# Low halves of all raw weights made by ScalarE and an adding transfer, and a recurrent branch with its steps in another order

## The chip, the cores and the metric

The kernel runs on one core of a Trainium2 chip. It uses TensorE (PE, with its weight loads shown apart as PEld), VectorE (DVE), ScalarE (ACT), GpSimd (POOL) and SyncE (SP). The metric is the device time of one launch in microseconds (us). Less is better.

## The reference, cut to what matters

One block of a decoder, in float32, over 1024 tokens and 16 meta tokens with 1024 features:

```
u = rms_norm(h)
q, k, v, r, a_lr, c_in, g_gla, g_conf = split(u @ w_in)      # 4 heads of 128 keys, 256 values
log_a = log_sigmoid(a_lr @ w_alpha_up + b_alpha) / 16
# recurrent branch, per head:
#   S_t = diag(exp(log_a_t)) S_{t-1} + k_t^T v_t ;  o_t = q_t S_t
o = rms_norm(o) * silu(r);                 br_gla  = o @ w_gla_o
c = silu(layer_norm(dwconv31(c1 * sigmoid(c2))));   br_conf = c @ w_conf_o
h = h + (sigmoid(g_gla) * br_gla + sigmoid(g_conf) * br_conf) @ w_out
a, b = split(rms_norm(h) @ w_up)                              # 2 x 2816
h = h + (silu(dwconv3(a)) * b) @ w_down
out = rms_norm(h)
```

Inside a chunk of tokens the recurrent branch needs the scores q_i k_j weighted by the decay between j and i. The kernel makes them by levels: at the level s, blocks of 2s tokens are taken, and the right half of each block (queries) meets the left half (keys), both scaled by the decay to the middle of the block.

## The kernel before, in words

**Three passes for one product.** Every large product is computed with numbers of reduced width. Each operand is the sum of a rounded part (high) and the rest (low), and a product takes three passes into the same accumulator: high weight by high activation (L187), high weight by low activation (L188), low weight by high activation (L189). Weights pass through as pieces of 128 x 1024 (512 KB), some of 512 or 768 columns: SP loads the raw piece (three buffers, `load_raw`), ACT rounds it into `wh` (L161, L174), and the rest goes to `wl`. The pairs `wh`, `wl` have three buffers too, so that a piece can be split only when the piece three before it has been used up.

**Two ways to the low half.** `split_w` subtracts on DVE (L162), or on POOL where it is asked to. The first 51 pieces of `w_mix` go another way (`load_w` with `PO`): ACT writes the rounded piece with its sign turned into `wl` (L173), and a transfer started by POOL adds the raw piece from memory to it (L175). POOL spends some 0.88 us on starting one.

**Stages.** From 0 to 740 us the 57 pieces of `w_mix` are multiplied; between these products, a count of steps per block (`tick`) lets the generators `gla` (recurrent branch, one head after the other), the convolution (most of DVE's work, L370) and later the layer norm advance. To 832 us come gate products and the layer norm. Then `w_gla_o` and `w_conf_o` follow (16 pieces, 11.3 us each), and from 1014 us `w_out` (8 pieces, twice, for two halves of the tokens, 5.7 us each). In the second half of `w_out`, the first half's tokens are normalised and become operands (`normalise`, `operand`; the low part on POOL, L228). The up-projection follows from 1108 us: 22 units, each with the pieces r1 and r2 of 1024 columns. A unit's two half-size blocks are combined by a fast multiplication scheme: sums of raw weights are made on POOL (L765 to L768) into `Pt` and r1, and the four pairs that a unit uses are `w1` (raw r1, for units from the fifth on), `w21` (from `Pt`), `w34` (from the changed r1; POOL subtracts from the fifth unit on) and the second half `a22` of r2. From 1577 us `w_down` closes the kernel: 24 pieces for each half of the tokens, with the units' results read back from memory by transfers that POOL starts (`ar`, L871) and split anew.

**What sets the order.** A scheduler places instructions in the order of the program, moved forward by `high_priority` for weights; each engine then goes through its row in order, and an instruction that waits holds back those behind it. That holds for the transfers that POOL starts as well.

**The recurrent branch.** Per head, `gla` makes the decays, then for each level s of 64, 32, 16 (band: L485, one product for each block) and 8, 4, 2, 1 (fine: L507, one 128 x 128 product for each of 8 chunks) the scaled tile `E` (`level`: subtraction on DVE for the keys L469 and POOL for the queries L470, an exponential on ACT, multiplication on DVE L472 and POOL L473). The product of a level stands one step behind its `level`. Fine products keep only the marked elements (`copy_predicated`, L511, one for each chunk). Then eight chunks follow one after the other: output, state, next chunk.

Of the kernel before, what the change touches and what calls it, by code (L numbers as in the profile page):

```python
# [11 lines left out]
F32R = mybir.dt.float32r  # L12
# [4 lines left out]
P = 128  # L17
# [47 lines left out]
def build(ctx, tc, xT, w_mix, w_o3, w_up, w_dn, w_au, pvec, masks, outT):  # L65
# [43 lines left out]
    def tmp512():  # L109
        return small([P, 520], "t512", bufs=6)  # L110
# [45 lines left out]
    def split_w(raw, eng=None):  # L156
        uid[0] += 1
        n = raw.shape[-1]
        hi = wspl.tile([P, 1024], F32R, tag="hi", name=f"wh_{uid[0]}")[:, :n]
        lo = wspl.tile([P, 1024], F32R, tag="lo", name=f"wl_{uid[0]}")[:, :n]  # L160
        pin(S.activation(hi, raw, AF.Copy))  # L161
        (eng or V).tensor_tensor(lo, raw, hi.bitcast(F32), op=ALU.subtract)  # L162
        return hi, lo

    def load_w(src, eng=None, ahead=4000):
        with tc.high_priority(offset=ahead):
            raw = load_raw(src)
            if eng is not PO:
                return split_w(raw, eng)
            uid[0] += 1  # L170
            hi = wspl.tile([P, 1024], F32R, tag="hi", name=f"wh_{uid[0]}")
            lo = wspl.tile([P, 1024], F32R, tag="lo", name=f"wl_{uid[0]}")
            pin(S.activation(lo, raw, AF.Copy, scale=-1.0))  # L173
            pin(S.activation(hi, raw, AF.Copy))  # L174
            nc.gpsimd.dma_start(lo, src, accum_op=ALU.add)  # L175
            return hi, lo
# [213 lines left out]
    def gla(h, q, k, vt):  # L390
# [32 lines left out]
        qd = slot(nm="qd")  # L423
        S.activation(qd[:, :SEQ], np_, AF.Exp, scale=-1.0 / TAU)
        V.memset(qd[:, :SEQ].rearrange("p (c t) -> p c t", t=CH)[:, :, 0:1], 1.0)
        V.tensor_tensor(qd[:, :SEQ], qd[:, :SEQ], qx, op=ALU.mult)
        yield 1
        km = small([P, 32], "km")
# [5 lines left out]
        pm = psumg()  # L434
        PE.matmul(pm[:15, 0:1], km[:, 16:31], q[:, 0:1], start=True, stop=True)
        PE.transpose(pm[:16, P : 2 * P], km[:, 0:16], ident)
        pms = small([16, 2], "pms")
        V.memset(pms, 0.0)  # L438
        V.tensor_copy(pms[:15, 0:1], pm[:15, 0:1])
# [3 lines left out]
        kmT = small([16, P], "kmT", bufs=1)  # L443
        S.activation(kmT, pm[:16, P : 2 * P], AF.Copy)
        po = psumg()
        PE.matmul(po[:, :DVH], kmT, vmeta, start=True, stop=True)
        st = small([P, DVH], "st", bufs=3)
        V.tensor_copy(st, po[:, :DVH])
        ss = small([P, NCH + 1], "ss")
        V.memset(ss, 1.0)  # L450
        yield 1
        kdT = slot(nm="kdT")
        for c4 in range(2):
            pt = psumg()
            for e in range(4):
                c = c4 * 4 + e
                PE.transpose(pt[:, e * P : (e + 1) * P], kd[:, c * CH : (c + 1) * CH], ident)
            S.activation(kdT[:, c4 * 512 : c4 * 512 + 512], pt, AF.Copy)
            yield 1
# [17 lines left out]
        for s in BANDS:  # L477
            X = level(s)
            yield 1
# [7 lines left out]
            for b in range(64 // s):  # L487
# [5 lines left out]
                else:  # L493
                    V.tensor_copy(dst, src)
            yield 1
        for n, s in enumerate(FINE):
            if s > 1:
                X = level(s)
                yield 1
                lt, rt = X, X  # L500
            else:
                lt, rt = kx, qx
            for c4 in range(2):
                pt = psumg()
                for e in range(4):
# [513 lines left out]
```

## Time and profile before

| what | value |
|---|---|
| median of 3 runs | 1852.41 us (1851.85 to 1853.7) |
| the profiled execution, its own time | 1854.06 us |
| its span, first to last instruction | 1852.3 us |
| mean granted TensorE clock | 0.989 of full speed |
| PE / DVE / ACT / POOL busy | 96% / 63% / 38% / 25% |
| DVE subtractions for `wl` (L162) | 134 instructions, 157.9 us |
| DMA share over the span | 26.6% (loads and stores by SP and ACT), 10.1% (started by POOL) |

How to read it: a busy share belongs to the whole span; what counts is where PE waits, since PE is busy for 1772.4 of 1852.3 us. An engine that is busy for less of the time than PE can still be the one that PE waits for, in one stage. The transfers have their own limit: the DMA share says how busy the core's 16 DMA engines were in a stretch.

### The profile page before, as it was taken

The numbers are of one execution on the slowest core, as the hardware profiler recorded it, in microseconds if no ns is written. First come the engines' busy times: TensorE is split into PE (matmuls) and PEld (weight loads), VectorE is DVE, ScalarE is ACT, GpSimd is POOL, SyncE is SP. The second block draws the span as 40 slices with busy tenths as digits, with TensorE's granted clock in tenths as the row PEclk, the third lists the DMA queues.
The fourth block names the chain that finished last, engine by engine and source line by source line (L and its number), as shares of the span: only waits on it lengthen the run. The fifth ranks groups of instructions, "written<-read, shape, count | busy, mean of one in ns | idle before, by whom it ended". The sixth has DMA issues, their size and how long they took to land.

```text
span 1852.3 us, 29073 instructions
## 1 busy us (share of the span) xinstructions
PE 1772.4 (96%) x12210; PEld 1688.0 (91%) x12210; DVE 1164.0 (63%) x1462; ACT 707.8 (38%) x1052; POOL 458.2 (25%) x333
## 2 busy tenths in 40 slices
PE   4999999999999999999999997999999999899997
PEld 3999899999899898999999997999999999677886
DVE  5239958969896761634365369877667766733523
ACT  5326426526435744592222343222222223423321
POOL 2102313413413422200000255433333334200000
PEclk8999999999999999999999998999999999999999
DMA  6343335244334553554133541221221224644532
GB/s 210 75 94 84 68 80 117 62 96 103 69 80 103 132 115 86 170 176 154 46 109 129 185 127 46 92 80 69 88 84 69 81 89 142 216 117 147 161 121 66
DMA packets 63443, 200.94 MB, mean 108 GB/s; under 512 B 6864, under 2 KB 14160, under 8 KB 63312
## 3 DMA queue, kind: packets, MB, share of 16 engines
q1 hardware_dynamic: 51168, 159.03, 26.6%
q0 software_dynamic: 10368, 37.75, 10.1%
q10 hardware_dynamic: 1776, 2.30, 0.4%
q8 instruction: 96, 1.57, 0.4%
q14 instruction: 35, 0.29, 0.0%
HBM read 162.31 MB, written 36.74 MB: 107 GB/s over the span
## 4 chain that ended last, share of the span: by engine, by line
PE 54%; DVE 5%; DMA 1%; issue 1%; ACT 1%; POOL 0%; DVEq 0%; ACTq 0%
PE prod L187 12%; PE prod L189 12%; PE prod L188 12%; PE mm L188 6%; PE mm L187 6%; PE mm L189 6%; DVE opl L228 1%; DVE wl L162 1%; DVE un L722 1%; DMA ar<-act_d 1%; PE g L943 1%; DMA wr<-in_w_dn 1%; DVE un L840 0%; DVE fy L825 0%; POOL opl L228 0%
## 5 line engine op out<-in xcount | busy, mean ns | idle before, releaser
L187 PE MATMUL mm<-uh,wh 128*128 128x342 f32 (+4 forms) x1344 | 444.8, 331 | 0.0
L188 PE MATMUL mm<-ul,wh 128*128 128x342 f32 (+4 forms) x1344 | 433.7, 323 | 0.0
L189 PE MATMUL mm<-uh,wl 128*128 128x342 f32 (+4 forms) x1344 | 432.1, 322 | 0.0
L188 PE MATMUL prod<-opl,wh 128*128 128x258 f32 x1232 | 350.2, 284 | 12.6 <-DVE opl L228 12.2
L187 PE MATMUL prod<-oph,wh 128*128 128x258 f32 x1232 | 350.5, 285 | 4.6 <-DVE t L805 3.5
L189 PE MATMUL prod<-oph,wl 128*128 128x258 f32 x1232 | 350.7, 285 | 0.0
L370 DVE SCALAR_TENSOR_TENSOR y<-c,pv,y 128x1026 f32<-128x1026 f32 x240 | 341.7, 1424 | 5.4 <-DVE pms L438 0.3
L161 ACT ACTIVATE wh<-wr 128x1024 fp32r<-128x1024 f32 (+2 forms) x152 | 147.8, 975 | 382.3 <-PE prod L188 175.3
L162 DVE TENSOR_TENSOR wl<-wr,wh 128x1024 fp32r<-128x1024 f32 (+2 forms) x134 | 157.9, 1181 | 176.4 <-ACT wh L161 175.1
L187 PEld LDWEIGHTS mm<-uh,wh 128*128 128x128 f32 x1344 | 255.0, 190 | 4.1 <-issue 2.1
L188 PEld LDWEIGHTS mm<-ul,wh 128*128 128x128 f32 x1344 | 254.7, 190 | 3.1 <-issue 2.1
L189 PEld LDWEIGHTS mm<-uh,wl 128*128 128x128 f32 x1344 | 255.1, 190 | 0.6 <-issue 0.3
L188 PEld LDWEIGHTS prod<-opl,wh 128*128 128x128 f32 x1232 | 235.1, 191 | 13.8 <-DVE opl L228 13.1
L187 PEld LDWEIGHTS prod<-oph,wh 128*128 128x128 f32 x1232 | 235.0, 191 | 5.7 <-issue 3.2
L189 PEld LDWEIGHTS prod<-oph,wl 128*128 128x128 f32 x1232 | 234.9, 191 | 0.0
L189 PE MATMUL mm<-oph,wl 128*128 128x512 f32 (+1 forms) x374 | 143.3, 384 | 4.2 <-DVE wl L162 4.2
L187 PE MATMUL mm<-oph,wh 128*128 128x512 f32 (+1 forms) x374 | 143.5, 384 | 2.1 <-ACT wh L161 1.3
L188 PE MATMUL mm<-opl,wh 128*128 128x512 f32 (+1 forms) x374 | 144.3, 386 | 0.6 <-DVE opl L228 0.6
L187 PE MATMUL prod<-sh,wh 128*128 128x342 f32 (+2 forms) x448 | 133.8, 299 | 0.5 <-ACT gate L629 0.5
L188 PE MATMUL prod<-sl,wh 128*128 128x342 f32 (+2 forms) x448 | 133.7, 298 | 0.0
L189 PE MATMUL prod<-sh,wl 128*128 128x342 f32 (+2 forms) x448 | 133.4, 298 | 0.0
L175 POOL DMA_DIRECT2D wl<-in_w_mix x50 | 43.8, 877 | 306.7 <-ACT wl L173 306.5
(239 smaller groups left out, 2873.2 us busy)
## 6 DMA issues: line engine op xcount, KB each, us to landing
wr<-in_w_mix SPq DMA_DIRECT2D x56, 512.0 KB, 3.9
wl<-in_w_mix POOLq DMA_DIRECT2D x50, 512.0 KB, 7.8
wr<-in_w_up SPq DMA_DIRECT2D x48, 512.0 KB, 3.3
wr<-in_w_o SPq DMA_DIRECT2D x32, 512.0 KB, 3.6
wr<-in_w_dn SPq DMA_DIRECT2D x32, 512.0 KB, 3.6
act_d<-fy SPq DMA_DIRECT2D x21, 512.0 KB, 2.6
ar<-act_d POOLq DMA_DIRECT2D x21, 512.0 KB, 6.9
wr<-in_w_dn SPq DMA_DIRECT2D x16, 384.0 KB, 3.1
```

Of the source, the lines that this page charges most:

```text
L161: pin(S.activation(hi, raw, AF.Copy))
L162: (eng or V).tensor_tensor(lo, raw, hi.bitcast(F32), op=ALU.subtract)
L175: nc.gpsimd.dma_start(lo, src, accum_op=ALU.add)
L187: PE.matmul(out, whi[:, wk], hi[:, c0:c1], start=first and k == 0, stop=False)
L188: PE.matmul(out, whi[:, wk], lo[:, c0:c1], start=False, stop=False)
L189: PE.matmul(out, wlo[:, wk], hi[:, c0:c1], start=False, stop=last and k == n - 1)
L228: (eng or V).tensor_tensor(lo, src, hi.bitcast(F32), op=ALU.subtract)
L370: V.scalar_tensor_tensor(y[:, :LQ], c[:, j : j + LQ], pcol("dw_w", i * CONV_K + j), y[:, :LQ], op0=ALU.mult, op1=ALU.add)
L722: V.scalar_tensor_tensor(pair_cols(un[hf][j], 0, width)[:, e], pair_cols(hh[j], 0, width)[:, e], pcol("ffn_g", 2 * j + e), rs[:, :width], ...
L943: PE.matmul(stats[c], ones, sq, start=n == 1, stop=n == KT - 1)
```

## The change

**Weights.** `load_w` now takes the second way for every piece. A new function `split_from` holds it: negated rounding and rounding on ACT (2 activations), then the adding transfer started by POOL. Besides all of `w_mix` it serves `w_gla_o`, `w_conf_o`, `w_out`, all pieces of `w_down`, and, in the up-projection, `w1` and `a22`, which are raw. `w21` and `w34` hold sums of weights and are still subtracted. In numbers of instructions DVE goes from 1160 rows to 1008, ACT from 1013 to 1142, POOL from 330 to 460; PE has 11332 for 11328.

**The recurrent branch.** `level` now runs some steps ahead of the product that uses it; the tile `qd` is made late; in the row of chunks the state advances two chunks ahead of the outputs. The fine products take only the 64 columns that count as the moving operand, the eight chunks share one bank, and one `copy_predicated` takes the place of eight.

```diff
-    def split_w(raw, eng=None):
+    def weight_pair(n):
         uid[0] += 1
-        n = raw.shape[-1]
         hi = wspl.tile([P, 1024], F32R, tag="hi", name=f"wh_{uid[0]}")[:, :n]
         lo = wspl.tile([P, 1024], F32R, tag="lo", name=f"wl_{uid[0]}")[:, :n]
+        return hi, lo
+
+    def split_w(raw, eng=None):
+        hi, lo = weight_pair(raw.shape[-1])
         pin(S.activation(hi, raw, AF.Copy))
         (eng or V).tensor_tensor(lo, raw, hi.bitcast(F32), op=ALU.subtract)
         return hi, lo
 
-    def load_w(src, eng=None, ahead=4000):
+    def split_from(src, raw):
+        hi, lo = weight_pair(raw.shape[-1])
+        pin(S.activation(lo, raw, AF.Copy, scale=-1.0))
+        pin(S.activation(hi, raw, AF.Copy))
+        nc.gpsimd.dma_start(lo, src, accum_op=ALU.add)
+        return hi, lo
+
+    def load_w(src, ahead=4000):
         with tc.high_priority(offset=ahead):
-            raw = load_raw(src)
-            if eng is not PO:
-                return split_w(raw, eng)
...
+            return split_from(src, load_raw(src))
...
-            wq.append(load_alpha(src) if src is w_alpha else load_w(src, PO if wpos[0] < 51 else V, rate["ahead"]))
+            wq.append(load_alpha(src) if src is w_alpha else load_w(src, rate["ahead"]))
...
+        def fine(n, s, lt, rt):
+            pt = psumg()
+            half = CH // 2
+            for c in range(NCH):
+                sl = slice(c * CH, (c + 1) * CH)
+                PE.matmul(pt[:, c * half : (c + 1) * half].rearrange("p (b t) -> p b t", t=s), lt[:, sl],
+                          right(rt[:, sl], s), start=True, stop=True)
+            mk = right(msk[:, n * CH : (n + 1) * CH], s).rearrange("p (o b) t -> p o b t", o=1)
+            V.copy_predicated(
+                Pc.rearrange("p c (b t) -> p c b t", t=2 * s)[:, :, :, s : 2 * s],
+                mk.broadcast_to([P, NCH, half // s, s]),
+                pt.rearrange("p (c b t) -> p c b t", t=s, b=half // s))
+
+        x64 = level(64)
...
+        x32 = level(32)
...
+        band(64, x64)
+        yield 1
+        x16 = level(16)
+        yield 1
+        band(32, x32)
...
+        x = level(8)
+        yield 1
+        band(16, x16)
+        yield 1
+        for n, s in enumerate(FINE[:-1]):
+            nxt = level(FINE[n + 1]) if n < 2 else None
+            yield 1
+            fine(n, s, x, x)
+            x = nxt
+            yield 1
...
+        for c in range(NCH + 2):
+            if c >= 2:
+                output(c - 2)
+            if c < NCH:
+                advance(c)
             yield 1
...
-            w1 = None if f < HEADS_UP else split_w(r1)
+            w1 = None if f < HEADS_UP else split_from(w_up[f], r1)
...
-            return w1, w21, w34, split_w(a22)
+            return w1, w21, w34, split_from(w_up[FT + f][:, 512:], a22)
```

**How instructions move: DVE in the recurrent branch.** First DVE's row before, where one head's levels 64, 32 and 16 (`E` of 128x8x64, 128x16x32, 128x32x16) are made among the convolution's steps (`y`), with the band products copied into `Pt`:

```order
L469 TENSOR_TENSOR E_2837<-nb_2525 128x8x64
L469 TENSOR_TENSOR E_2882<-nb_2525 128x16x32
...
L472 TENSOR_TENSOR E_2882<-E_2882,k_1139 128x16x32
L370 SCALAR_TENSOR_TENSOR y_2888<-c_1954,pv,y_2888 128x1026 x4
L494 COPY Pt<-g_2872 64x8x64
L370 SCALAR_TENSOR_TENSOR y_2888<-c_1954,pv,y_2888 128x1026 x3
L494 COPY Pt<-g_2925 32x8x32
L469 TENSOR_TENSOR E_2972<-nb_2525 128x32x16
L469 TENSOR_TENSOR E_3043<-nb_2525 128x64x8
L370 SCALAR_TENSOR_TENSOR y_2888<-c_1954,pv,y_2888 128x1026
L472 TENSOR_TENSOR E_2972<-E_2972,k_1139 128x32x16
```

And the same place of the changed kernel:

```order
L443 TENSOR_TENSOR E_2765<-nb_2493 128x16x32
...
L443 TENSOR_TENSOR E_2846<-nb_2493 128x32x16
L368 TENSOR_SCALAR y_2877<-c_1960,pv 128x1026
L446 TENSOR_TENSOR E_2765<-E_2765,k_1139 128x16x32
L371 SCALAR_TENSOR_TENSOR y_2877<-c_1960,pv,y_2877 128x1026
L446 TENSOR_TENSOR E_2846<-E_2846,k_1139 128x32x16
L371 SCALAR_TENSOR_TENSOR y_2877<-c_1960,pv,y_2877 128x1026
L467 COPY Pt<-g_2807 64x8x64
L371 SCALAR_TENSOR_TENSOR y_2877<-c_1960,pv,y_2877 128x1026 x3
L467 COPY Pt<-g_2852 32x8x32
```

The tile of level 16 stood behind the copies of levels 64 and 32; now it is made ahead of both.

**POOL in the last up-projection unit and at the entry to `w_down`.** Before, the unit's sums (`Pt`, `wr`) and its subtraction, then the read-back transfers `ar` in one row, and two low halves of activations (`opl`):

```order
L768 TENSOR_TENSOR wr_14796<-wr_14796,Pt 128x512
L162 TENSOR_TENSOR wl_14813<-wr_14796,wh_14812 128x1024
L871 DMA ar_15205<-act_d_10272 128x2x512
...
L871 DMA ar_15265<-act_d_10280 128x2x512
L228 TENSOR_TENSOR opl_15268<-ar_15265,oph_15267 128x1024
L871 DMA ar_15271<-act_d_10281 128x2x512
L228 TENSOR_TENSOR opl_15274<-ar_15271,oph_15273 128x1024
```

And in the changed kernel, from the same sums on:

```order
L796 TENSOR_TENSOR wr_14748<-wr_14748,Pt 128x512
L165 TENSOR_TENSOR wl_14766<-wr_14748,wh_14765 128x1024
L172 DMA wl_14770<-in_w_up 128x512
L899 DMA ar_15159<-act_d_10182 128x2x512
...
L172 DMA wl_15174<-in_w_dn 128x1024
...
L172 DMA wl_15205<-in_w_dn 128x1024
L899 DMA ar_15215<-act_d_10189 128x2x512
L899 DMA ar_15221<-act_d_10190 128x2x512
L229 TENSOR_TENSOR opl_15224<-ar_15221,oph_15223 128x1024
L899 DMA ar_15227<-act_d_10191 128x2x512
L229 TENSOR_TENSOR opl_15230<-ar_15227,oph_15229 128x1024
L172 DMA wl_15236<-in_w_dn 128x1024
```

The adding transfers of the first two pieces of `w_down` stand between the read-backs, and that of the third behind both subtractions of activations.

## Rows read from the trace of the kernel before

**Rows 1.** PE's waits: what for, total us, times, longest us.
```profile
PE prod L188 <- DVE opl L228: 12.2, 4, 6.2
PE g L485 <- POOL E L473: 10.0, 4, 4.6
...
PE g L550 <- DVE t L544: 4.6, 4, 1.7
PE mm L189 <- DVE wl L162: 4.2, 3, 1.9
PE prod L187 <- DVE t L805: 3.5, 4, 0.9
...
PE g L507 <- DVE E L472: 2.6, 2, 1.7
PE g L435 <- DVE km L433: 1.4, 1, 1.4
```

**Rows 2.** Window behind a recurrent wait: busy PE, PEld, DVE, ACT, POOL, PEclk, DMA.
```profile
200.00:204.00 4.00, 4.00 (x76) 3.96 (x77) 3.96 (x4) 0.27 (x1) 4.00 (x3) 0.57 0.59 146
```

**Rows 3.** PE's instructions: start, duration, engine, line, what.
```profile
31.39 0.41 PE L189 MATMUL mm<-uh,wl 128*128 128x242 f32 x1
31.60 0.41 PE L187 MATMUL mm<-uh,wh 128*128 128x242 f32 x1
...
206.05 1.05 PE L507 MATMUL g<-E 128*128 128x128 f32 x8
```

**Rows 4.** Adding transfer by itself: POOL's start of it, its landing after that.
```profile
L175 POOL DMA_DIRECT2D wl<-in_w_mix x1: 862/862/862, 170.5 to 170.5; - x1
...
DMA to landing us min/median/max: 5.2/5.2/5.2
```

**Rows 5.** The same beside a raw load, and the page's medians (section 6).
```profile
L175 POOL DMA_DIRECT2D wl<-in_w_mix x1: 880/880/880, 184.0 to 184.0; - x1
...
DMA to landing us min/median/max: 7.9/7.9/7.9
...
wl<-in_w_mix POOLq DMA_DIRECT2D x50, 512.0 KB, 7.8
```

**Rows 6.** ACT and a window (columns as Rows 2) at the entry to w_gla_o.
```profile
837.80 1.99 ACT L161 ACTIVATE wh<-wr 128x1024 fp32r<-128x1024 f32 x2
...
840.00:845.00 5.00, 5.00 (x34) 5.00 (x34) 3.37 (x6) 1.06 (x1) 0.00 (x0) 1.00 0.94 308
```

**Rows 7.** POOL and PE while the first half is normalised inside w_out.
```profile
1081.46 5.79 POOL L228 TENSOR_TENSOR opl<-un,oph 128x1032 fp32r<-128x1032 f32 x2 [1.74 <-ACT oph L227]
...
1085.45 0.36 PE L187 MATMUL prod<-mh,wh 128*128 128x258 f32 x1 [0.36 <-DVE hh L745]
```

**Rows 8.** ACT in one up-projection unit, and DMA of the same stretch.
```profile
1406.23 1.06 ACT L161 ACTIVATE wh<-wr 128x1024 fp32r<-128x1024 f32 x1 [2.27 <-PE prod L188]
...
1414.86 1.06 ACT L161 ACTIVATE wh<-wr 128x1024 fp32r<-128x1024 f32 x1 [1.77 <-PE prod L188]
...
1409.00:1411.00 2.00, 2.00 (x19) 2.00 (x18) 1.39 (x2) 0.00 (x0) 2.00 (x2) 1.00 0.00 0
```

**Rows 9.** Entry to w_down: read-backs' landings (first nine; tenth), POOL, PE.
```profile
DMA to landing us min/median/max: 5.4/8.9/11.3
...
DMA to landing us min/median/max: 4.2/4.2/4.2
...
1572.72 0.72 POOL L871 DMA_DIRECT2D ar<-act_d  x1 [2.03 <-PE prod L188]
1581.38 3.35 POOL L228 TENSOR_TENSOR opl<-ar,oph 128x1024 fp32r<-128x1024 f32 x1 [7.94 <-ACT oph L227]
...
1596.95 0.50 PE L189 MATMUL mm<-oph,wl 128*128 128x512 f32 x1 [1.90 <-DVE wl L162]
```

**Rows 10.** ACT in w_down: each start follows the end of a 768-column piece.
```profile
1641.25 1.06 ACT L161 ACTIVATE wh<-wr 128x1024 fp32r<-128x1024 f32 x1 [4.75 <-PE mm L188]
1645.38 1.06 ACT L161 ACTIVATE wh<-wr 128x1024 fp32r<-128x1024 f32 x1 [3.07 <-PE mm L188]
```

More of the change, by code (lines that the diff above doesn't have):

```diff
@@ L476, in gla, with band @@
         Pc = Pt.rearrange("p (c t) -> p c t", t=CH)
-        for s in BANDS:
-            X = level(s)
-            yield 1
+        def band(s, X):
             pt = psumg()
@@ L494, in gla, with right @@
                     V.tensor_copy(dst, src)
[L495 to L514 removed]
+        def right(t, s):
+            return t.rearrange("p (b t) -> p b t", t=2 * s)[:, :, s : 2 * s]
@@ new lines, in gla @@
+        x64 = level(64)
+        kdT = slot(nm="kdT")
+        for c4 in range(2):
+            pt = psumg()
+            for e in range(4):
+                c = c4 * 4 + e
+                PE.transpose(pt[:, e * P : (e + 1) * P], kd[:, c * CH : (c + 1) * CH], ident)
+            S.activation(kdT[:, c4 * 512 : c4 * 512 + 512], pt, AF.Copy)
+            yield 1
+        x32 = level(32)
+        pm = psumg()
+        PE.matmul(pm[:15, 0:1], km[:, 16:31], q[:, 0:1], start=True, stop=True)
+        PE.transpose(pm[:16, P : 2 * P], km[:, 0:16], ident)
@@ new lines, in gla @@
+        pms = small([16, 2], "pms")
+        V.memset(pms, 0.0)
+        V.tensor_copy(pms[:15, 0:1], pm[:15, 0:1])
+        kmT = small([16, P], "kmT", bufs=1)
+        S.activation(kmT, pm[:16, P : 2 * P], AF.Copy)
+        yield 1
[4 more added lines that the diff above has]
+        band(32, x32)
+        po = psumg()
+        PE.matmul(po[:, :DVH], kmT, vmeta, start=True, stop=True)
+        st = small([P, DVH], "st", bufs=4)
+        V.tensor_copy(st, po[:, :DVH])
@@ L516, in gla, with advance @@
+        V.tensor_tensor(qd[:, :SEQ], qd[:, :SEQ], qx, op=ALU.mult)
+        fine(3, 1, kx, qx)
+        yield 1
         o = [slot(nm="o"), slot(nm="o")]
-        for c in range(NCH):
-            op = psumg()
-            PE.matmul(op[:, :DVH], qd[:, c * CH : (c + 1) * CH], st, start=True, stop=False)
-            PE.matmul(op[:, :DVH], Pt[:, c * CH : (c + 1) * CH], vc(c), start=False, stop=True)
+        sts = [st]
+        def advance(c):
             kv_ps = psumg()
             PE.matmul(kv_ps[:, :DVH], kdT[:, c * CH : (c + 1) * CH], vc(c), start=True, stop=True)
-            st2 = small([P, DVH], "st", bufs=3)
-            V.scalar_tensor_tensor(st2, st, dec[:, c : c + 1], kv_ps[:, :DVH], op0=ALU.mult, op1=ALU.add)
-            st = st2
+            st2 = small([P, DVH], "st", bufs=4)
+            V.scalar_tensor_tensor(st2, sts[-1], dec[:, c : c + 1], kv_ps[:, :DVH], op0=ALU.mult, op1=ALU.add)
+            sts.append(st2)
@@ L526, in gla, with output @@
+        def output(c):
+            op = psumg()
+            PE.matmul(op[:, :DVH], qd[:, c * CH : (c + 1) * CH], sts[c], start=True, stop=False)
+            PE.matmul(op[:, :DVH], Pt[:, c * CH : (c + 1) * CH], vc(c), start=False, stop=True)
             oc = o[c // 4][:, (c % 4) * DVH : (c % 4 + 1) * DVH]
@@ L545, in gla @@
         yield 1
+        yield 1
         for d in range(2):
@@ L556, in gla @@
                 S.activation(og[:, 1 + c4 * 512 : 1 + c4 * 512 + 512], pt, AF.Copy, scale=gcol)
+            pt = psumg()
+            PE.transpose(pt[:, 0:2], om[:, d * P : (d + 1) * P], ident[:2, :2])
+            S.activation(og[:, 0 : LQ : LQ - 1], pt[:, 0:2], AF.Copy, scale=gcol)
             ogs[2 * h + d] = og
```

59 lines of the change are left out of this document (10 added, 49 removed).

## Prediction

> **What bounds the kernel now.** The page's first part says PE: busy for 1772.4 of 1852.3 us, at a clock that was granted almost in full. A gain can only come out of PE's waits, or of fewer or shorter passes; a loss comes from each piece of weights whose low half arrives after PE asks for it. So I read the list of PE's waits first [rows 1]. The recurrent branch holds four of them (L485, L550, L507, L435): 10.0 + 4.6 + 2.6 + 1.4 = 18.6 us. The entry to the up-projection holds 12.2 us behind the low halves of activations (L228), its first units 3.5 us (L805). The waits for `wl` itself, which is what the change moves off DVE, come to 4.2 us in all, three of them, all at the entry to `w_down`. So the low halves are nearly free today. The reader is to see that 130 subtractions leave an engine that PE hardly waits for, and that what replaces them has a longer way.
>
> That way is priced next. A DVE subtraction of a 1024-column piece takes some 1.2 us after `wh`. The adding transfer, already in use for most of `w_mix`, lands 5.2 us after its start when nothing else moves [rows 4], 7.9 us beside a raw load, and 7.8 us in the median of 50 [rows 5]. In `w_mix` a piece is used for over 11 us and this is hidden. Elsewhere I go through the stages one by one and ask when the low half is wanted.
>
> **Recurrent branch.** Making the level tiles earlier takes away the wait for `E` (10.0 + 2.6), and the late moves of `km` and the output's tail take away most of the other 6.0. Behind the longest of these waits the clock stood at 0.57 for 4 us [rows 2]; 0.43 x 4 = 1.7 us came back late there and would be saved too. At most this is 18.6 + 1.7 = 20.3 us. I take -15, since POOL makes half of each `E` in 2.3 us steps and has no fewer of them, and the chunks' own chain keeps some of its waits. Ends: -20 and -8 (only L485's waits go).
>
> **Fine products.** 128 products (four heads, four levels, eight chunks) of 128 columns become 128 of 64. In float32 each is two passes, 256 in all. Eight passes take 1.05 us [rows 3]: less some 0.28 for the last one, 0.11 us from start to start. If columns decided, half of it would go, 256 x 0.055 = 14 us. But the same group of rows has passes of 242 columns at the low clock 0.21 us apart, which is more than 242 columns at 1.2 GHz (0.202): there something else than columns sets the pace, and all have a 128-column weight load in common. At the full clock that floor would be half, 0.105, and the fine passes already stand on it. I take 0, ends 0 and -14. The Trainium skill, "TensorE: Matmul & The Clock Gate", section "LDWEIGHTS (loading the stationary operand)", speaks against this part of the change: a load costs its columns over 1.2 in ns, 107 ns for 128, whatever the moving operand is. No run here shows a full-clock pass of 64 columns on 128 columns of weight; by that rule the term is 0. The 112 predicated copies saved are DVE time, which PE does not wait for in this stage.
>
> **Entry to the up-projection and its first units.** DVE loses a 512-column subtraction for each unit there, under 1 us at each of some six places where PE waits for DVE (12.2 + 3.5 us in eight waits [rows 1]). I take -6.5; ends 0 and -8.
>
> **Entry to `w_gla_o`.** ACT comes to the second piece at 837.80 behind 16 activations of inputs [rows 6]. Its negated rounding ends at 838.9, the transfer starts, and the DMA engines are 0.94 busy there [rows 6], so the 7.9 us of the crowded case holds: 846.8. The second piece starts 11.3 us after the first, at 843.2, and wants its low half at 843.4. That is +3.4; ends +2 and +5.
>
> **Normalising inside `w_out`.** Three low operands now stand on POOL ahead of a transfer. The third begins with the pair at 1081.46 and one lasts 2.9 us [rows 7], so the transfer starts at 1084.4 and lands at 1089.6, alone as it then is. PE starts that piece at 1085.45 and wants the low half 0.3 us later: +4; ends +2 and +7. In the rest of `w_out` a piece lasts 5.7 us and two pieces lie between the release of a pair and its use: 11.4 us, against 2 x 1.06 for ACT and 7.9 for the transfer, 10.0. It holds; 0, upper end +8 (0.5 us for each of 16).
>
> **Up-projection units from the fifth on.** `wh` of the next `w1` is made at 1406.23 [rows 8]. The second activation ends at 1408.3, and the transfer starts then. The unit that uses it starts at 1414.86 or so, with the low half wanted 0.3 us later, at 1415.2. That leaves 6.9 us. The DMA engines are idle from 1409 on [rows 8], so I take the landing of rows 4, 5.2: 1413.5, on time by 1.7 us. The term is 0 and the cover is the rest of the unit before; if it lands in 7.9 as in rows 5, PE stands for 1.0 us in each of 18 units, +18. POOL's starts, 0.9 us each, delay its sums of weights, which have 4 us of idle time ahead of them.
>
> **Entry to `w_down`.** Here POOL's row decides, as the order shows: two transfers of low halves stand between the read-backs, the third behind both subtractions of activations. Worked through: the last `a22` is started at about 1563.3, the first three read-backs land 8.9 us later [rows 9], ACT splits them, and the first piece's transfer starts at 1573. Four more read-backs follow until 1576.5; the second piece stands behind their split on ACT and starts at 1584.4. The ninth read-back starts at 1586 (at 1572.72 before) and lands after 5 to 7 us, near 1592. ACT takes 1.06 for the high half, POOL 3.35 for the low one [rows 9]: 1596.4. Only then the tenth starts, 0.72 + 4.2 [rows 9]: 1601.3; ACT and POOL again: 1605. Now the third piece's transfer starts and lands 5.2 us later, at 1610, where PE asked for it at 1596.95 before [rows 9], a wait included. That is 13; I take +12, ends +5 (every read-back lands in 4.2) and +16 (7.9 for the last transfer).
>
> **The rest of `w_down`.** Pieces of 768 columns last 1645.38 - 1641.25 = 4.1 us [rows 10]. Where two of them follow each other, three times in a half, the piece that takes the freed pair has 2 x 4.13 = 8.3 us for two activations (2.1) and the transfer (7.9) less the two passes that do without the low half (0.46): 9.5. That is 1.2 x 6 = +7; ends 0 (5.2 alone) and +15. At the second half's entry eleven read-backs share the queue with the transfers: +2, ends 0 and +8.
>
> **Sum.** -15 + 0 - 6.5 + 3.4 + 4 + 0 + 0 + 12 + 7 + 2 = +6.9. The profiled execution took 1854.06 us, 1.76 more than its span; so 1861.0 for an execution like it. The median of the runs is 1.65 below that execution: 1859.3, rounded to 1860.
>
> **Rivals.** First, *the gains come in full and the queue is short*: the recurrent branch gives -20, the units' DVE work -8, the entry to `w_down` costs +5, its steady part 0, the other places +9: -14, so 1838; with part of the fine products' 14, below that. For it: PE's waits in the recurrent branch are real and all are behind work that is now made earlier. Against it: the order of POOL's row at 1577 us is a fact of the program. Second, *the transfer lands in 7.9 in the up-projection too*: +18 on the forecast, 1878. It decides at a landing of 6.9 us. For it: 7.8 is the median of rows 5. Against it: those fifty mostly start within a microsecond of a raw load, and here the engines are idle. Third, *the low half arrives fast everywhere*: a landing of some 3 us would end the losses at `w_gla_o` and in `w_down`'s steady part, and cut 2 us at each of two other places: 6.9 - 3.4 - 7 - 4 = -7.5, so 1845. Against it stands each landing in rows 4 and 5. The Trainium skill, "DMA: Bandwidth & Descriptors", section "Anatomy of one DMA — SWDGE (gpsimd) path", gives 2.0 us and the bytes over 436 GB/s for such a transfer, 3.2 us for 512 KB. The trace does not agree (5.2 alone), and the measurement decides. Fourth, *gain and loss cancel*: within 0.2% (3.7 us, about what a measurement of this kernel can tell from no change).
>
> **How the numbers follow.** Forecast, slower by 4 to 22 us: 0.46. Second rival: 0.13. First: 0.20; third: 0.07. Fourth: 0.14. Hence slower 0.59, the same 0.14, faster 0.27. The likeliest case by itself reaches from 1856 to 1874. The range from 1836 to 1884 takes in the first and third rival and most of the second, and leaves out fine products at their full 14 and a `w_down` at all upper ends.
>
> **What would show it.** In the profile after: PE's waits for `E` (level) gone or a third of 10.0; fine products with starts still 0.11 apart; a new entry in PE's waits, `mm` on L190 (the third pass after the change) released by the transfer of `wl`, with some 12 us near 1600 and 1.2 us three times a half; one `prod` wait of 4 us near 1070 to 1090 and one of 3 us near 840; no wait on `wl` between 1213 and 1577. I am wrong if the units of the up-projection take more than 20.2 us each, if the fine products become clearly shorter, or if PE meets no wait for `wl` at 1600.

## Result, and the profile after

The changed kernel takes 1901.58 us in the median of four runs (1899.05 to 1909.78); the kernel before 1852.56 beside it. The ratio is 1.0265 (95% interval 1.0242 to 1.0289): slower, by 49 us where 8 were forecast, and outside the range that ended at 1884. The profiled execution has a span of 1898.1 us, 45.8 more than before.

Where the time went is read from the stages' ends. The next lines are from the trace of the kernel before, the products that read the operands of three stages: count, duration in ns (min/median/max), first and last start in us. `sh` is the operand of `w_gla_o` and `w_conf_o`, `mh` that of `w_out`, `oph` in this line that of `w_down`.

```profile
L187 PE MATMUL prod<-sh,wh x448: 279/285/426, 831.9 to 1013.7; 128*128 128x342 f32 x64, 128*128 128x258 f32 x64, 128*128 128x252 f32 x22
L187 PE MATMUL prod<-mh,wh x256: 276/283/470, 1014.0 to 1108.0; 128*128 128x258 f32 x96, 128*128 128x252 f32 x32
L187 PE MATMUL mm<-oph,wh x374: 274/392/628, 1578.1 to 1840.2; 128*128 128x512 f32 x165, 128*128 128x256 f32 x22
```

The same of the changed kernel:

```profile
L188 PE MATMUL prod<-sh,wh x448: 277/286/491, 824.4 to 1013.7; 128*128 128x342 f32 x64, 128*128 128x258 f32 x64, 128*128 128x252 f32 x22
L188 PE MATMUL prod<-mh,wh x256: 275/283/472, 1014.1 to 1117.3; 128*128 128x258 f32 x96, 128*128 128x252 f32 x32
L188 PE MATMUL mm<-oph,wh x374: 274/393/796, 1590.5 to 1886.0; 128*128 128x512 f32 x165, 128*128 128x256 f32 x22
```

From such lines comes this table of stage lengths in us, for one profiled execution of each kernel. The stages follow without a gap: to the first product of `w_gla_o`; from there to the first of `w_out`; `w_out` from first to last; from there to the first of `w_down`; `w_down` from first to last; the rest.

| kernel | recurrent, mix, gates | w_gla_o, w_conf_o | w_out | up-projection | w_down | rest | span |
|---|---|---|---|---|---|---|---|
| before | 831.9 | 182.1 | 94.0 | 470.1 | 262.1 | 12.1 | 1852.3 |
| changed | 824.4 | 189.7 | 103.2 | 473.2 | 295.5 | 12.1 | 1898.1 |
| difference | -7.5 | +7.6 | +9.2 | +3.1 | +33.4 | 0 | +45.8 |
| e1: recurrent branch alone | 825.1 | 182.3 | 94.4 | 469.3 | 261.9 | 12.1 | 1845.1 |
| e2: weights alone | 835.6 | 190.5 | 103.5 | 469.6 | 298.3 | 12.0 | 1909.5 |
| e3: w_down by DVE | 823.5 | 189.8 | 103.2 | 472.5 | 261.9 | 12.1 | 1863.0 |
| e4: w_o by DVE | 826.7 | 182.3 | 94.4 | 471.4 | 298.6 | 12.0 | 1885.4 |
| e13: few bytes | 826.7 | 183.6 | 100.2 | 469.9 | 277.7 | 12.5 | 1870.6 |

The up-projection's +3.1 is uncertain: ten more kernels below treat the weights of that stage in the same way, and it takes 469.6 (e2) to 473.0 us (e9) there, 471.3 in the mean of the eleven, against 470.1 before.

The list of PE's waits of the changed kernel answers to [rows 1]:

```profile
PE mm L190 <- DMA wl<-in_w_dn: 19.2, 8, 8.0
...
PE prod L190 <- DMA wl<-in_w_o: 9.3, 2, 5.3
...
PE prod L189 <- DVE opl L229: 8.3, 3, 3.9
PE mm L188 <- ACT wh L171: 6.0, 1, 6.0
PE g L477 <- DVE E L446: 5.7, 4, 2.5
PE g L580 <- DVE o L570: 4.2, 4, 1.1
PE prod L188 <- DVE t L833: 3.5, 4, 0.9
PE g L971 <- DVE t L970: 2.8, 1, 2.8
PE prod L190 <- DMA wl<-in_w_up: 2.3, 1, 2.3
```

The 4.2 us for `wl` have become 19.2 + 9.3 + 2.3 behind transfers, and 6.0 behind ACT, which now makes the high half late too. But PE's idle time grew only by 23.8 us (1898.1 - 1794.4 against 1852.3 - 1772.4). The other 22.0 are busy time: as many matmuls as before (12210), some at the low clock. By stages, in the order of the table, PE's idle time changed by -8.7, +5.3, +4.7, -0.9 and +23.5 us, its busy time by +1.2, +2.3, +4.5, +4.0 and +9.9. The windows show the low clock behind the waits of three stages (columns: length; busy time of PE, PEld, DVE, ACT, POOL; PEclk, DMA share, GB/s):

```profile
840.00:845.00 5.00, 3.49 (x12) 3.49 (x13) 0.00 (x0) 0.00 (x0) 0.00 (x0) 0.50 1.06 279
...
1090.00:1095.00 5.00, 2.78 (x13) 2.78 (x14) 0.00 (x0) 0.89 (x2) 3.71 (x5) 0.64 1.02 279
...
1635.00:1640.00 5.00, 5.00 (x18) 4.00 (x17) 0.00 (x0) 0.41 (x1) 0.00 (x0) 0.75 1.04 316
```

The DMA engines are full in all three. The page's section 3 (packets, MB, share of 16 engines) and section 6 (KB each, median us to landing) of the changed kernel:

```profile
q0 software_dynamic: 29088, 98.05, 27.7%
q1 hardware_dynamic: 51168, 159.03, 26.0%
...
wl<-in_w_o POOLq DMA_DIRECT2D x32, 512.0 KB, 8.1
...
wl<-in_w_dn POOLq DMA_DIRECT2D x32, 512.0 KB, 7.2
wl<-in_w_up POOLq DMA_DIRECT2D x22, 512.0 KB, 5.5
```

POOL's queue carried 37.75 MB for 10.1% of the span before; now 98.05 MB for 27.7%. In the traces DVE's instructions fell from 1462 to 1220, by 130 subtractions of weights and 112 copies of the recurrent branch.

### The profile page after: what moved, and what is told of

Its sections match the earlier page's. It is cut to its first block, busy times and chain, and to the rows that moved or that the text cites. A ratio compares the mean times of both kernels' runs of the same rounds, so it can differ in the third digit from the quotient of the medians.

```text
span 1898.1 us, 29147 instructions
## 1 busy us (share of the span) xinstructions
PE 1794.4 (95%) x12210; PEld 1705.0 (90%) x12210; DVE 1013.1 (53%) x1220; ACT 815.2 (43%) x1180; POOL 545.6 (29%) x463
## 3 DMA queue, kind: packets, MB, share of 16 engines
q0 software_dynamic: 29088, 98.05, 27.7%
q1 hardware_dynamic: 51168, 159.03, 26.0%
q8 instruction: 96, 1.57, 0.3%
## 4 chain that ended last, share of the span: by engine, by line
PE 72%; DVE 10%; issue 8%; DMA 6%; POOL 2%; ACT 2%; SPq 0%; DVEq 0%; POOLq 0%; ACTq 0%
PE prod L190 12%; PE prod L188 12%; PE prod L189 11%; PE mm L190 10%; PE mm L188 10%; PE mm L189 10%; DVE y L371 5%; DMA ar<-act_d 2%; DMA wl<-in_w_dn 1%; PE g L477 1%; DMA wl<-in_w_o 1%; POOL wl L172 1%; DMA x<-in_xT 1%; DVE E L446 1%; PE g L545 1%
## 5 line engine op out<-in xcount | busy, mean ns | idle before, releaser
L171 ACT ACTIVATE wh<-wr 128x1024 fp32r<-128x1024 f32 (+1 forms) x180 | 177.2, 986 | 433.2 <-issue 192.5
L170 ACT ACTIVATE wl<-wr 128x1024 fp32r<-128x1024 f32 (+1 forms) x180 | 174.7, 972 | 21.1 <-PE mm L190 21.0
L172 POOL DMA_DIRECT2D wl<-in_w_mix x56 | 49.3, 881 | 408.4 <-ACT wl L170 354.5
L190 PE MATMUL mm<-oph,wl 128*128 128x512 f32 (+1 forms) x374 | 147.7, 395 | 19.2 <-DMA wl<-in_w_dn 19.2
L188 PE MATMUL mm<-oph,wh 128*128 128x512 f32 (+1 forms) x374 | 147.6, 395 | 6.9 <-ACT wh L171 6.0
```

Source lines behind the costliest of these rows:

```text
L188: PE.matmul(out, whi[:, wk], hi[:, c0:c1], start=first and k == 0, stop=False)
L190: PE.matmul(out, wlo[:, wk], hi[:, c0:c1], start=False, stop=last and k == n - 1)
```

## Experiments

Medians, and ratios to the kernel before with their 95% intervals.

**e1 and e2: one half of the change each.** e1 has the new `gla` on the kernel before, e2 the new weights with the old `gla`:

```diff
 # e1, on the kernel before: gla() as in the change, load_w() and split_w() as they were
-        for s in BANDS:
-            X = level(s)
...
+        x64 = level(64)
...
+        band(64, x64)
...
 # e2, on the changed kernel: gla() as before, split_from() as in the change
+        for s in BANDS:
+            X = level(s)
...
-        x64 = level(64)
```

> The kernel before with the recurrent branch of the changed kernel (order of its steps and halved fine products), all weights as before. Theory: stage times of the changed kernel add up, and the recurrent branch is what moved the first product of w_gla_o from 831.9 to 824.4, so this kernel takes 7.5 us less, about 1845 (1842 to 1848). Rival: the branch gives the 15 us of the prediction, and the last six pieces of w_mix with their adding transfers and the second activation in the gate stage took half of it back: about 1837.

> The changed kernel with the recurrent branch of the kernel before: all raw weights by the adding transfer and nothing else. Theory: the loss of the weights is 7.6 (w_gla_o, w_conf_o) + 9.2 (w_out) + 3 (up-projection) + 33.5 (w_down) = 53, so about 1906. Rival: the two parts hurt each other in w_mix (both use POOL's row), so that the weights by themselves cost clearly less, 1895 or below.

e1 took 1846.97 us, ratio 0.9966 (0.9952 to 0.9979); e2 1910.68, 1.0312 (1.0297 to 1.0326). Both rivals fall. By the medians the branch is worth 5 us without the new weights (1852.16 - 1846.97) and 9 with them (1910.68 - 1901.58), and the weights cost 58.5 without it and 54.6 with it, some 5 more than the 53 that e2's theory added up. Most of the 4 us between lie ahead of `w_gla_o`: e2's time up to there is 3.7 us longer than before, while e1's and the changed kernel's are nearly equal.

In e1 the waits that remain of the 18.6 us are two (list of PE's waits, 150 to 745 us):

```profile
PE g L476 <- DVE E L445: 5.4, 3, 2.5
PE g L579 <- DVE o L569: 4.2, 4, 1.1
```

9.0 us of waits went, and the stage is 6.8 us shorter. The wait for a tile `E` moved from level 16 and POOL to DVE: level 8 in the first head (2.5 us) and level 2 in the next two. And the clock still falls behind it: 0.50 in 200 to 205, where the kernel before had 0.66. PE's busy time up to `w_gla_o` is 3.2 us longer than before.

**e10 and e11: which part of the branch.** e10 asks for level 8 a step earlier; e11 keeps the fine products on 128 columns, with a copy for each chunk.

```diff
 # e10, on e1
         x16 = level(16)
         yield 1
+        x = level(8)
+        yield 1
         band(32, x32)
...
-        x = level(8)
-        yield 1
 # e11, on e1: in fine()
-                PE.matmul(pt[:, c * half : (c + 1) * half].rearrange("p (b t) -> p b t", t=s), lt[:, sl],
-                          right(rt[:, sl], s), start=True, stop=True)
...
+                    PE.matmul(pt[:, e * CH : (e + 1) * CH], lt[:, sl], rt[:, sl], start=True, stop=True)
...
+                    V.copy_predicated(right(Pt[:, sl], s), mk, right(pt[:, e * CH : (e + 1) * CH], s))
```

> The recurrent branch alone (weights as in the kernel before) with level 8 asked for one step ahead of the product of level 32. Theory: PE's remaining wait for the tile of level 8 (5.4 us in three heads, with the low clock behind it) goes: 1841 to 1844. Rival: DVE is full in that stretch (49.1 of 50 us busy from 150 to 200), so the wait moves to another tile: 1846 to 1849.

> The recurrent branch alone in its new order, but with the fine products on all 128 columns and one predicated copy for each chunk, as before. Theory: 16 halved passes take 1.89 us and 16 full ones took 1.95, so halving gives PE 1 us in all; the time is that of the branch with halved products, 1847, or up to 3 us more where the 112 extra copies on DVE make the tiles late. Rival: the 5 us gain of the branch comes from DVE's lighter copies alone, and the order gives nothing: 1852.

e10: 1846.96 us, 0.9964 (0.9951 to 0.9976). The rival holds, with its reason: PE no longer waits for the tile of level 8, but for that of level 2, the third of a head's four groups of fine products, 6.0 us in all. The longest of these waits (PE, start, duration, wait in brackets):

```profile
216.11 3.03 PE L476 MATMUL g<-E 128*128 128x64 f32 x16 [4.46 <-DVE E L445]
```

e11: 1847.19, 0.996 (0.9947 to 0.9972): the halved products and the single copies are worth nothing that can be measured, and the order of the steps is all of the gain. The passes themselves say so. Sixteen in the kernel before, then sixteen halved ones in e1 (start, duration):

```profile
374.31 1.95 PE L507 MATMUL g<-E 128*128 128x128 f32 x16
```
```profile
367.69 1.90 PE L476 MATMUL g<-q,k 128*128 128x64 f32 x16
```

**e3 and e4: one stage's weights back to DVE.**

```diff
     def load_w(src, ahead=4000):
         with tc.high_priority(offset=ahead):
-            return split_from(src, load_raw(src))
+            raw = load_raw(src)
 # e3, with rate["sub"] set ahead of w_down
+            return split_w(raw) if rate.get("sub") else split_from(src, raw)
 # e4, with rate["down"] set ahead of w_down
+            return split_w(raw) if len(order) <= wpos[0] < len(order) + 32 and not rate.get("down") else split_from(src, raw)
```

> The changed kernel with the low halves of w_down by a DVE subtraction again. Theory: the 33.5 us that w_down got longer (295.8 for 262.3 from its first product to its last) come from the low halves' transfers in POOL's row between the read-backs, and go away: about 1868, with the third piece of w_down asked for some 19 us after the first product, as before. Rival: the read-backs are late because the transfers of the up-projection still stand ahead of them, or the low clock stays: half of the loss or more remains, 1884 or above.

> The changed kernel with the low halves of w_gla_o, w_conf_o and w_out by a DVE subtraction again. Theory: the 16.8 us that these stages got longer go away: about 1885. Rival: part of that time is ACT's, which stood late at the entry for the splits of inputs and not for the transfer, or DVE's in w_out: 1893 or above.

e3: 1865.33 us, 1.0070 (1.0056 to 1.0084). e4: 1886.87, 1.0182 (1.0168 to 1.0196). Both theories hold. The table's columns for these stages go back to their old lengths within 0.4 us and the others stay within some 3, so the loss is each stage's own.

**e8: the up-projection alone, on the kernel before.**

```diff
-            w1 = None if f < HEADS_UP else split_w(r1)
+            w1 = None if f < HEADS_UP else split_from(w_up[f], r1)
...
-            return w1, w21, w34, split_w(a22)
+            return w1, w21, w34, split_from(w_up[FT + f][:, 512:], a22)
```

> The kernel before with only the up-projection changed: w1 and the second half of r2 by the adding transfer. Theory: it lands in 5.5 us in these units, in time, so no unit from the fifth on gets longer, and the entry to the up-projection gains at most 2 us from DVE's lighter load: 1850 to 1853. Rival: the first units lose at their first transfer (2.3 us in the changed kernel) and through the low clock after it, which the changed kernel shows as 3 us from the first up-projection product to the first of w_down: 1855 or above.

e8: 1855.63 us, 1.0014 (1.0005 to 1.0023). The number is the rival's, but the kernel before took 1853.47 in the median of the same runs, so that the loss is some 2 us, between the cases. Its profiled execution has a span of 1851.4 and 470.9 us for the up-projection (470.1 before), but it is one of the fastest of e8's eleven (1853.22): no gain from the lighter DVE and no loss in the units from the fifth on.

**e5, e6, e7, e12: the entry to `w_down`.**

```diff
 # e5: read-backs started by SP
-        nc.gpsimd.dma_start(raw[:, :1024].rearrange("p (e t) -> p e t", t=512), src)
+        nc.sync.dma_start(raw[:, :1024].rearrange("p (e t) -> p e t", t=512), src)
 # e6: no subtraction of activations on POOL there
-        return operand(raw, 1024, PO if hf == 0 and j in (8, 9) else V)
+        return operand(raw, 1024, V)
 # e7, in load_w; rate["down"] is set to len(order) + 3 ahead of w_down; in e12 to len(order) + 10
+            return split_w(raw) if wpos[0] < rate.get("down", 0) else split_from(src, raw)
```

> The changed kernel with the read-backs of w_down's activations started by SP in place of POOL. Theory: the entry to w_down is late (third piece's low half 40.9 us after the first product, 18.8 before) because read-backs and adding transfers stand in one row on POOL and share one queue, each group 10 to 13 us behind the last; on SP's queue the read-backs land in 3 to 4 us beside it, the chain gets some 15 us shorter, and the kernel takes about 1886 (1880 to 1890). Rival: the DMA engines are full (share 0.9 to 1.0 there) and the bytes take their time by either queue: 1895 or above.

> The changed kernel with the low halves of the ninth and tenth read-back made by DVE in place of POOL, so that no subtraction stands ahead of the third piece's transfer in POOL's row. Theory: the two took 2.8 and 2.3 us of POOL on the chain, and the tenth read-back's start stood behind the first of them; together with the low clock some 8 to 11 us go, about 1892. Rival: the landings of the read-backs alone decide (8 to 10 us each, the third transfer stands behind the tenth split on ACT in any case): within 3 us of the changed kernel, 1899 or above.

> The changed kernel with the first three pieces of w_down split by DVE and the other 45 by the adding transfer. Theory: the entry holds 22 of the 33.5 us, so the kernel takes about 1879 (1876 to 1884), and the rest of w_down stays 11 us longer than before. Rival: what stalls is the steady part, with its DMA share of 0.85 to 1.0, and the entry only moves it: 1890 or above.

> The changed kernel with the first ten pieces of w_down split by DVE, the other 38 by the adding transfer. Theory: what is lost is the entry, where read-backs, the last unit's results and raw pieces share the DMA engines, and whichever adding transfers come first there are late (with three pieces by DVE it was the fourth); with ten pieces the read-backs are done, and w_down loses only about 6 us: 1873 (1870 to 1877). Rival: a full row of adding transfers keeps the DMA engines at 0.85 to 1.0 for the whole of w_down, and the loss moves on to the eleventh piece: 1884 or above.

e5: 1893.16 us, 1.0218 (1.0204 to 1.0232). e6: 1901.46, 1.0254 (1.0238 to 1.0270). e7: 1891.08, 1.0200 (1.0187 to 1.0214). e12: 1879.48, 1.0138 (1.0125 to 1.0152). Against the changed kernel's 1901.58 that is 8 us, nothing, 10 and 22. e5 lies between its two cases. In e6 the time is the rival's, but not the reason. With the subtractions off POOL the low half of the third piece is used 30.6 us after the first product (1589.44), 40.9 in the changed kernel; POOL's two subtractions did hold it up by 10.3 us. The fourth piece then waits too, and is used at 40.6. PE's first passes on the low halves of both:

```profile
1620.08 0.80 PE L190 MATMUL mm<-oph,wl 128*128 128x512 f32 x1 [5.33 <-DMA wl<-in_w_dn]
...
1629.99 0.53 PE L190 MATMUL mm<-oph,wl 128*128 128x512 f32 x1 [2.05 <-DMA wl<-in_w_dn]
```

Of the 10.3 us 3.0 are left at the end of `w_down` in this execution, and the medians show nothing. In e7 the time is the rival's as well, though e12 below speaks against its reason. The first three pieces are early now, and the fourth, the first that is added, makes PE wait:

```profile
1622.09 0.79 PE L191 MATMUL mm<-oph,wl 128*128 128x512 f32 x1 [5.04 <-DMA wl<-in_w_dn]
```

In e12 the time lies between the cases, but the eleventh piece does not wait for its low half. These are PE's waits on transfers, from the first product of `w_down` on, in three places of the second half, two of them at the piece that follows two pieces of 768 columns:

```profile
PE mm L191 <- DMA wl<-in_w_dn: 4.3, 3, 2.1
```

PE's timeline shows where each kernel loses. The table has the us from the first product of `w_down` to the next pass after 50, 150, 520 and 1100 of its 1122 passes; the pass after 50 is the first on the third piece's low half, and the second half of the tokens begins after 528.

| kernel | 50 | 150 | 520 | 1100 |
|---|---|---|---|---|
| before | 18.8 | 45.2 | 133.2 | 259.9 |
| changed | 40.9 | 71.8 | 161.7 | 293.3 |
| e6 | 30.6 | 66.0 | 156.1 | 290.2 |
| e7 | 18.8 | 60.0 | 151.1 | 284.8 |
| e12 | 22.4 | 49.1 | 137.4 | 275.1 |
| e13 (below) | 33.4 | 59.9 | 148.2 | 275.5 |

In e12 PE is 4.2 us behind the kernel before after 520 passes, hardly more than after 150 (3.9), though added pieces are in use from the eleventh on. The other 11 come in the second half: 4.0 at its entry, under the sums for the last norm, and 6.6 around the three waits above. So adding pieces in a row hold for a long stretch, and the loss sits in single places. (Its first ten pieces took longer than e3's: POOL's subtraction for the ninth read-back took 6.85 us in e12 and 2.86 in e3, and four subtractions of DVE at the same time 4.62 and 6.83. I did not follow this up.)

**e9: PE kept busy where it waits.** 88 products whose results nobody reads, in four groups about as long as the waits:

```diff
+    def fill(times):
...
+                pin(PE.matmul(junk[:, :512], hi[:, :P], hi[:, :512], start=t == 0, stop=t == times - 1))
...
+    seen, count, warm = set(), [0], [(0, 12), (0, 22), (22, 32), (0, 0)]
...
+            fill(idle[0])
...
+            fill(idle[1])
```

> The changed kernel with 88 idle products at the entry to w_down (12 ahead of the first piece's first low pass, 22 ahead of the second's, 22 ahead of the third piece, 32 ahead of its first low pass), whose result is not used, so that PE is busy where it waited; they are about as long as the waits. Theory: the waits stay, but the low clock behind them goes, which I put at some 10 us of the 33.5 in w_down (granted clock 0.50 to 0.76 in 1595 to 1640 of the changed kernel): about 1893 (1890 to 1896). Rival: the clock costs nothing there, since PE would wait for the next piece all the same: 1900 or above.

e9: 1903.25 us, 1.0274 (1.0255 to 1.0292). The fillers did what they were to do: the clock in e9 stays at 1.00 where the changed kernel had 0.50 (window of 5 us):

```profile
1595.00:1600.00 5.00, 4.62 (x19) 3.11 (x17) 0.54 (x1) 1.33 (x2) 0.00 (x0) 1.00 1.02 399
```

Over the 40.9 us from the first product on the mean was 0.92 for 0.70. And `w_down` took 296.5 us, as long as without them (295.5); the third piece's low pass came 1.6 us later. The rival holds: at this entry the chain of low halves sets the time, and passes at the full clock only reach the next wait sooner. At the entries of `w_gla_o` and `w_out`, where one wait is followed by many pieces without another, the clock's cost stays; there it was not tried with fillers.

**e13: the same transfers with a sixteenth of the bytes.** The adding transfers of `w_gla_o`, `w_conf_o`, `w_out` and `w_down` bring only 64 columns of a piece, so this kernel leaves most of the low halves out and serves for its time alone. The order of the rows is as in the change.

```diff
-        nc.gpsimd.dma_start(lo, src, accum_op=ALU.add)
+        m = few or raw.shape[-1]
+        nc.gpsimd.dma_start(lo[:, :m], src[:, :m], accum_op=ALU.add)
...
-            return split_from(src, load_raw(src))
+            return split_from(src, load_raw(src), 64 if wpos[0] >= len(order) else None)
```

> The changed kernel with the adding transfers of w_gla_o, w_conf_o, w_out and w_down cut to the first 64 columns of each piece (a sixteenth of the bytes; the other columns of the low halves keep the negated high part, so the output is not the reference's). Starts, waits and order stay. Theory A, bytes: the low halves are late because 512 KB more for each piece fill the DMA engines (share 0.9 to 1.0 at the entries); then most of the 33.5 us of w_down and of the 16.8 us before go, about 1865. Theory B, the chain: what counts is that a transfer stands in POOL's row behind waits, and waits for ACT twice; then a shorter landing gives some 4 us at each hop of the entry to w_down, and about 1885 remains.

e13: 1871.08 us, 1.0095 (1.0069 to 1.0120), between the two. The last row of the table of stages splits it. `w_gla_o` with `w_conf_o` is at 183.6: 1.5 of its 7.6 us stay, so the loss is mostly bytes. `w_out` is at 100.2: 6.2 of 9.2 stay, two thirds. `w_down` is at 277.7: 15.6 of 33.4 stay, nearly half. What stays is the chain, with what a small transfer still takes to land (4.2 to 6.1 us at the entries). The entry of `w_down` in POOL's row follows, first the changed kernel (first product of `w_down` at 1590.49), with PE's third piece at the end:

```profile
1587.60 0.91 POOL L172 DMA_DIRECT2D wl<-in_w_dn  x1 [8.96 <-ACT wl L170]
1588.21 2.83 POOL L899 DMA_DIRECT2D ar<-act_d  x4
1601.24 0.91 POOL L172 DMA_DIRECT2D wl<-in_w_dn  x1 [10.20 <-ACT wl L170]
...
1612.03 2.84 POOL L229 TENSOR_TENSOR opl<-ar,oph 128x1024 fp32r<-128x1024 f32 x1 [8.69 <-ACT oph L228]
...
1622.55 0.94 POOL L172 DMA_DIRECT2D wl<-in_w_dn  x1
...
1631.37 0.80 PE L190 MATMUL mm<-oph,wl 128*128 128x512 f32 x1 [8.03 <-DMA wl<-in_w_dn]
```

and e13 (first product at 1580.43):

```profile
1577.27 0.91 POOL L173 DMA_DIRECT2D wl<-in_w_dn  x1 [8.71 <-ACT wl L170]
...
1588.79 0.91 POOL L173 DMA_DIRECT2D wl<-in_w_dn  x1 [8.08 <-ACT wl L170]
...
1597.21 2.85 POOL L230 TENSOR_TENSOR opl<-ar,oph 128x1024 fp32r<-128x1024 f32 x1 [6.32 <-ACT oph L229]
...
1607.77 0.92 POOL L173 DMA_DIRECT2D wl<-in_w_dn  x1
...
1613.86 0.80 PE L191 MATMUL mm<-oph,wl 128*128 128x512 f32 x1 [5.31 <-DMA wl<-in_w_dn]
```

The third piece's low half is used 40.9 us after the first product in the changed kernel, 33.4 in e13, and 18.8 before [rows 9]. So 14.6 us of the entry come from the order (a transfer behind read-backs, behind ACT, behind POOL's own subtractions, the last worth 10.3 by e6) and 7.5 more from the bytes: the second transfer starts 13.6 us after the first, and 11.5 in e13, and the third lands after 8.8 us, and 6.0 in e13. And behind the entry e13 loses only 1 us more to the end of `w_down`, where the changed kernel loses 11: that part is bytes.

No version tried is measurably faster than e1 with its 1846.97 us.

## Why the prediction was wrong, step by step

The direction and the places were right, the size was not: +6.9 was summed where the span grew by 45.8. The 38.9 us between are 7.5 in the recurrent branch, 9.6 in the up-projection, 4.2 in `w_gla_o`, 5.2 in `w_out` and 12.4 in `w_down`. Two steps failed: the landing times, taken from a trace with few adding transfers, and the price of a wait of PE, which left out the low clock behind it.

- **Recurrent branch** (-15 taken, ends -20 and -8): -7.5, and -6.8 alone. Three steps failed: that the earlier tiles take away the wait for `E`, that "the late moves of `km` and the output's tail take away most of the other 6.0", and the gain in clock. Of 12.6 us for `E` 5.7 stayed, now behind DVE, for levels 8 and 2; of the other 6.0 the tail's 4.2 stayed; and the clock fell again. DVE was 49 of 50 us busy in that stretch, before and after; this was in the windows and I did not use it.
- **Fine products** (0, ends 0 and -14): right. 1.90 us against 1.95 for sixteen, and no difference in e11. The Trainium skill, "TensorE: Matmul & The Clock Gate", section "LDWEIGHTS (loading the stationary operand)", gives the load of a weight as its columns over 1.2 in ns, 107 ns for 128 columns, with no term for the moving operand. The trace agrees: 0.11 us a pass with 64 moving columns, where halving would have given 0.06.
- **Entry to the up-projection** (-6.5): +3.1, and +1 over all kernels with this edit. The step that failed is that less work for DVE shortens PE's waits behind it. DVE was busy for 5.6 us less in the first 110 us of the stage (89.6 for 95.2), but the wait behind it only fell from 12.2 to 8.3 us, to 10.1 in e8 and 10.5 in e2; a first adding transfer came late by 2.3, and 4.0 us more of busy time came up. Alone (e8) the edit costs 2 us by the medians.
- **`w_gla_o`** (+3.4): the wait was 5.3, since the transfer landed after 9.8 us, not 7.9, and the stage lost 7.6. **Normalising in `w_out`** (+4): the wait was 4.0, and the stage lost 9.2. That the wait is the forecast one is luck: the transfer landed after 7.0 us, not 5.2, but PE also asked 2.5 us later, held up by a wait of 1.9 behind DVE (`hh`) and the low clock behind that. The wait was priced in both, and what follows it was not: the clock granted afterwards, 0.50 for 5 us in `w_gla_o` and 0.64 to 0.70 for 15 in `w_out`, with 2.3 and 4.5 us more of busy time. I had read in [rows 2] that 4 us at 0.57 follow a wait of the recurrent branch and used it as a gain; I did not carry it to the waits that I added.
- **Units from the fifth on** (0, rival +18): right, no wait; landing 5.5 us in the median, close to the 5.2 of [rows 4]. A unit took 20.23 us on PE, 20.16 before and 20.20 in e1 with the old weights, so the 20.2 that was named as a sign of being wrong could not tell one case from the other.
- **Entry to `w_down`** (+12, end +16): +22 (40.9 for 18.8). The step that failed is the landing: I let the ninth read-back land after 5 to 7 us and the second transfer start 11.4 behind the first. The ninth took 8.3, near the 8.9 that [rows 9] had shown, the hop 13.6, and the last transfer 8.8 instead of 5.2. The chain itself was about right: with few bytes it gives 14.6, where 13 had been worked out.
- **The rest of `w_down`** (+9): 33.4 - 22 = 11. The size was near by luck. Pieces that follow two of 768 columns do wait, as forecast, but the low halves cost PE 0.3 to 1.1 us in five places, 3.1 in all and not 7. The largest part was not forecast: 4.5 us are lost up to pass 150, around the sums for the last norm (L971, 2.8 us behind DVE).

**The range.** The upper ends of my own terms, without the rival of the units, add up to -8 + 0 + 0 + 5 + 7 + 8 + 16 + 15 + 8 = 51, which is 1903 in the median. I took it as unlikely that they come together. But those of the transfers were not independent: each held a landing time, taken from a trace in which POOL's queue was 10.1% of the engines' time, and the change itself makes it 27.7%. One cause moved these landings in one direction: 9.8 for 7.9, 7.0 for 5.2, 8.8 for 5.2. That is not all of the miss: the low clock was in no term of the transfers, and the two gains fell short mostly for other reasons than landings.

**The rival of fast landings** was also judged rightly: the lowest median of the adding transfers of the changed kernel is 5.5 us. What the Trainium skill states in "DMA: Bandwidth & Descriptors", section "Anatomy of one DMA — SWDGE (gpsimd) path", 3.2 us by its sum, is not what these runs show for transfers that add.

What stays open: why the adding transfers of the last six pieces of `w_mix` cost e2 3.7 us and the changed kernel nothing that shows; how much of the loss in `w_gla_o` and `w_out` fillers for PE would give back; and what another order of ACT's row would do at the entry to `w_down`, where the roundings of weights stand behind those of read-backs (8.6 us of PE's waits in e13 are for high halves from ACT).

## What to carry to other kernels

Work that left an engine PE hardly waited for gained nothing here, and a transfer in its place cost at the points where its result is the first thing wanted: entries of stages more than their steady part. Price such a transfer in the DMA load that the change itself makes, and add to each new wait of PE the low clock that follows it, unless another wait follows at once. A piece that comes earlier is a gain only if the next one comes earlier too: e6 freed 10.3 us at the third piece and kept 3. Terms that rest on one unknown, here a landing time, belong at their ends together when the range is drawn.

## What the runs showed of the hardware that I had not expected

- An adding transfer holds the DMA engines longer than a load of the same size. From section 3 of the two pages: the added 60.3 MB took 27.7% of 1898.1 us less 10.1% of 1852.3 us, 339 us of all 16 engines, 178 GB/s; the hardware queue moved 159.03 MB in 26.0% of 1898.1 us, 322 GB/s. The trace of the kernel before shows it in a calm stretch too, 168 to 210 us, where POOL's queue held three adding transfers and nothing else: 1.57 MB in 23.1% of 42 us, 162 GB/s, beside 2.10 MB in 17.7%, 282 GB/s, on the hardware queue.

```profile
q0 software_dynamic: 432, 1.57, 23.1%
q1 hardware_dynamic: 576, 2.10, 17.7%
...
wl<-in_w_mix POOLq DMA_DIRECT2D x3, 512.0 KB, 5.6
```

- Read-backs that POOL starts in a row land late, with or without additions between them: the first ten, of 512 KB each, took 8.2 us in the median in the changed kernel and 6.8 in e13, where the additions are small, but 8.7 before, where none stands between them. The tenth, started alone, took 4.2 both before and in the changed kernel.
- At the entry to `w_down`, keeping the clock up where PE waits gave nothing (e9): in this stage the low granted clock was no cost, because what PE waits for, and not PE, set the time.
